# All eight x tiles of block 1 by DMA transpose, W1 stores spread over ten units, the sums of W1 tile 6 later in their period

## The chip, the cores and the metric

The kernel runs on one core of one Trainium2 chip. The metric is the device time of one execution in microseconds (us). A profile is one such execution, and its span, from the first to the last instruction, is about 1.8 us shorter than the time. Engines: PE (TensorE matmul), PEld (its weight loads), DVE (VectorE), ACT (ScalarE), POOL (GpSimd), SP (SyncE, which here only issues DMAs).

## The reference

```python
batch, m, k, h, n = 16, 512, 768, 3072, 768        # all float32
y = np.matmul(x, w1) + b1
y = 0.5 * y * (1.0 + erf(y / np.sqrt(2.0)))
return np.matmul(y, w2)
```

## The kernel before

The 8192 rows of x are worked in eight blocks of 1024 rows. Both matrix products use Strassen's scheme in its Winograd form: seven products of half-size blocks in place of eight, at the price of sums of operands on DVE. The first product goes unit by unit: unit (block, k) makes one pair of 128-wide column strips of the hidden layer. Blocks 0 and 1 are interleaved, since W1 is read from memory, cast and summed only once, and the finished W1 tiles (raw and summed, 672 KB each) are stored to DRAM for the later blocks. The order of units is:

```python
seq = ([(0, k) for k in range(7)] +
       [(1, 0), (1, 1), (1, 2), (0, 7), (1, 3), (0, 8), (1, 4), (0, 9), (1, 6), ...])
at = {u: n for n, u in enumerate(seq)}             # position; at[1, 0] is 7
```

Each position is one period of about 4.5 us. Within it, PE works on the unit `i` that starts and on the unit `j` before it, and calls `fill(slot)` between products. DVE executes in the order in which the program emits, so a slot decides what stands ahead of what:

```python
def period(i, j, fill):                            # cut
    p1(i, 0, i.C); copy_xy(i)                      # PE into bX; ACT
    p7(j)                                          # PE into bY, then DVE add (L613)
    fill(1)
    p5(i)                                          # PE into bW; ACT copy
    fill(2)
    p3(j)                                          # PE into bZ, then DVE add (L641)
    fill(3)
    p6(i)                                          # PE into bY, then DVE copy bY to bZ (L659)
    j.right_done(); fill(4)
    p4(j); fill(5)
    p2(i); fill(6)
```

The next period's `p7` accumulates in the same bY, so PE can't start it before the copy at L659 has read bY.

The sums wait in a list, `soon`. `sums(ns)` emits from its front as many as fit a budget, and slot 6 emits the rest. The parts that the change touches:

```python
X1_PE = (3, 7)                                     # these two x tiles are transposed on PE
X1_AT = ((5, 2), (6, 1))                           # at (position, slot)

KEEP = {at[1, 0]: range(7), at[0, 7] + 1: (7,), at[0, 8]: (8,), at[0, 9]: (9,), ...}

def transposes_a(pos):
    for t in (pos - 1, pos + 3):
        if t not in X1_PE:
            transpose_dma(1, t)                    # SP issues it (L305)

def fill_a(pos, slot):                             # cut
    if (pos, slot) in X1_AT:
        transpose_pe(1, X1_PE[X1_AT.index((pos, slot))])
    if pos == at[1, 0] - 1 and slot == 2:
        x_sums(1, soon, slice(RH // 2, RH), (0, 1))          # second half of the columns
    if slot == (1 if pos < at[1, 0] else 4) and pos + 1 < len(seq) and seq[pos + 1][0] == 0:
        prep_wt(seq[pos + 1][1])                   # four sums of the next W1 tile
    if slot == 1:
        if pos == at[1, 0] - 2:
            x_sums(1, soon, slice(0, RH // 2), (0, 1))       # first half: tiles 0, 1, 4, 5
    ...
    elif slot in (1, 2, 4, 5):
        sums((0, 600, 300, 0, 600, 300)[slot])
    if slot == 5:
        loads_a(pos)                               # POOL issues loads of W1, W2 and x
        if pos < 5:
            transposes_a(pos)
        for n in KEEP.get(pos, ()):
            keep(n)                                # SP stores W1 tile n (L225)
    if slot == 6:
        flush(soon)
```

Of the kernel before, what the change touches and what calls it, by code (L numbers as in the profile page):

```python
# [10 lines left out]
P = 128  # L11
# [11 lines left out]
def kernel(  # L23
# [8 lines left out]
    nc = tc.nc  # L32
    B, M, K = x.shape
# [6 lines left out]
    KQ = K // P // 2  # L40
# [48 lines left out]
    def cut(off, n, pattern=None, **dims):  # L89
        ap = arena[:, off:off + n]  # L90
        return ap.rearrange(pattern, **dims) if pattern else ap
# [94 lines left out]
    with tc.manual_schedule():  # L186
# [9 lines left out]
        def sums(ns):  # L196

            for q in (soon, queue):
                while q and ns >= q[0][0] * 0.6:
                    ns -= q[0][0]  # L200
                    q.pop(0)[1]()
# [25 lines left out]
        def prep_wt(n, ks=()):  # L227
            o = {s: w1_op(wts[n], s) for s in range(7)}
            early = ((T3, B22, T1, SUB), (T2, T3, B11, ADD), (T4, B21, T2, SUB), (T1, T1, B11, SUB))
            usual = ((T3, B22, T1, SUB), (T1, T1, B11, SUB), (T2, B22, T1, SUB), (T4, B21, T2, SUB))  # L230
            for d, a, b, op in [early[k] for k in ks] if ks else usual:
                later(KQ * P, lambda d=d, a=a, b=b, op=op: tt(o[d], o[a], o[b], op), soon)
# [6 lines left out]
        def prep_w2(d, c, q):  # L239
            a, b = {T1: (T3, B11), T2: (B22, T1), T3: (B22, T3), T4: (B21, T2)}[d]  # L240
            o = [w2v[s][:, :, c:c + W2C, :] for s in (d, a, b)]
            later(2 * W2C * N4, lambda: tt(*o, SUB), q)
# [47 lines left out]
        xhs = {}  # L290

        def xh_of(sb, t):
            if sb < ONE:
                return cut(sb * GR + GR // 2 + t * K, K)
            return xh_late[t % 3]
# [5 lines left out]
        def xT_of(sb, t):  # L301
            return XTs[sb][:, t // NU, :, (t % NU) * P:(t % NU + 1) * P]

        def transpose_dma(sb, t):
            nc.sync.dma_start_transpose(out=xT_of(sb, t), in_=xhs[t])  # L305

        def copy_halves(out, in_):
            for c in (slice(0, KQ), slice(KQ, 2 * KQ)):
                nc.scalar.copy(out=out[:, c, :], in_=in_[:, c, :])

        def transpose_pe(sb, t, copy=nc.scalar.copy):
            for kc in range(2 * KQ):
                nc.tensor.transpose(out=bT[t % 2][:, kc, :], in_=xhs[t][:, kc * P:(kc + 1) * P],
                                    identity=ident[:])
            copy(out=xT_of(sb, t), in_=bT[t % 2][:])
# [5 lines left out]
        def x_sums(sb, q, r=slice(0, RH), ks=range(4)):  # L321
            A11, A12, A21, A22 = [a[:, :, r] for a in blocks(sb)]
            S1, S2, S4 = [a[:, :, r] for a in XSs[sb]]
            n = KQ * len(range(RH)[r])
            ops = ((S1, A21, A22, ADD), (S2, S1, A11, SUB), (A21, A11, A21, SUB), (S4, A12, S2, SUB))
            for k in ks:
                later(n, lambda k=k: tt(*ops[k]), q)

        def g_sum(k, U, c0=0, c1=NH, q=None):
            G1, G2 = g_of(U // NU)  # L330
            r = slice(U % NU * P, (U % NU + 1) * P)
            g11, g21 = G1[:, c0:c1, 0, r], G1[:, c0:c1, 1, r]
            g12, g22 = G2[:, c0:c1, 0, r], G2[:, c0:c1, 1, r]
            s = [t[:, c0:c1, :] for t in GS]
            a, b, op = ((g21, g22, ADD), (s[0], g11, SUB), (g11, g21, SUB), (g12, s[1], SUB))[k]
            later((c1 - c0) * P, lambda: tt(s[k], a, b, op), q)
# [376 lines left out]
        xf = cut(GR, 8 * K).bitcast(FP32).rearrange("p (t k) -> p t k", t=4)  # L713
# [23 lines left out]
        def spin(n):  # L737

            for k in range(n):
                nc.tensor.matmul(out=(bX[1], bY[1])[k % 2][:], lhsT=zero[:, 0, 0:P], rhs=zero[:, 0, :],  # L740
                                 start=True, stop=True, skip_group_check=True)

        spin(9)
        for t in range(4):
            xhs[t] = xh_of(0, t)
            nc.vector.tensor_copy(out=xhs[t], in_=xf[:, t, :])
            transpose_pe(0, t, copy_halves if t == 3 else nc.scalar.copy)
            if t == 0:
                nc.tensor.transpose(out=bW[:, 0:2 * NH], in_=bf, identity=idf[0:2 * NH, 0:2 * NH])
                nc.scalar.copy(out=b1t[:], in_=bW[:, 0:2 * NH])  # L750
            spin(2)
# [7 lines left out]
        def plain(n, row, side, half, r=slice(0, RH)):  # L759
            slot = ((B11, T1), (B21, B22))[half][side]  # L760
            for c in range(KQ):
                nc.tensor.matmul(out=banks[n, row][side][:, r], lhsT=w1_op(wts[n], slot)[:, c, :],
                                 rhs=blocks(0)[2 * row + half][:, c, r],
                                 start=half == 0 and c == 0 and r.start == 0,
                                 stop=half == 1 and c == KQ - 1, skip_group_check=True)

        def plain_done(n, row, side):
            nc.scalar.activation(out=Gs[0][side][:, n, row, :], in_=banks[n, row][side][:, 0:RH],
                                 func=GELU, bias=b1t[:, 2 * n + side:2 * n + side + 1])
# [41 lines left out]
        for k in (2, 3):  # L811
            for r in (top, bottom):
# [5 lines left out]
        seq = ([(0, k) for k in range(7)] +  # L818
               [(1, 0), (1, 1), (1, 2), (0, 7), (1, 3), (0, 8), (1, 4), (0, 9), (1, 6), (0, 10), (0, 11),
                (1, 5), (1, 10), (1, 11), (1, 7), (1, 8), (1, 9)])  # L820
        at = {u: n for n, u in enumerate(seq)}
# [10 lines left out]
        def loads_a(pos):  # L832
            if pos == 0:
                load_wt(4)
                load_next_x(1, (0, 4, 1, 5))
                load_wt(5)
                load_next_x(1, (2, 6, 3, 7))
                load_wt(6)
            for n in range(7, NH):
                if pos == at[1, over[n]] + 1:  # L840
                    load_wt(n)
            if pos in w2_at_pos:
                load_w2(*w2_at_pos[pos])

        X1_PE = (3, 7)
        X1_AT = ((5, 2), (6, 1))

        KEEP = {at[1, 0]: range(7), at[0, 7] + 1: (7,), at[0, 8]: (8,), at[0, 9]: (9,), at[0, 10]: (10,), at[0, 11]: (11,)}

        def transposes_a(pos):  # L850
            for t in (pos - 1, pos + 3):
                if t not in X1_PE:
                    transpose_dma(1, t)

        def fill_a(pos, slot):
            if pos == 2 and slot == 1:
                plain(1, 1, 1, 1, bottom)
                plain_done(1, 1, 1)
            if (pos, slot) in X1_AT:
                transpose_pe(1, X1_PE[X1_AT.index((pos, slot))])  # L860
            if pos == at[1, 0] - 1 and slot == 2:
                x_sums(1, soon, slice(RH // 2, RH), (0, 1))
            if slot == (1 if pos < at[1, 0] else 4) and pos + 1 < len(seq) and seq[pos + 1][0] == 0:
                prep_wt(seq[pos + 1][1])
            if slot == 4:
                if pos in (3, 4):
                    prep_wt(pos - 3, (3,))
                for m, c in ((21, 9), (22, 0), (23, 3), (23, 6)):
                    if pos == m:
                        prep_w2(T2, c, queue)  # L870
                        prep_w2(T3, c, late if m == 23 else queue)
                if pos == 23:
                    for c in range(0, NH, W2C):
                        prep_w2(T4, c, late)
            if slot == 1:
                if pos == at[1, 0] - 2:
                    x_sums(1, soon, slice(0, RH // 2), (0, 1))
                if pos == at[1, 0]:
                    x_sums(1, soon, ks=(2, 3))
                if pos == at[0, NH - 1] + 2:  # L880
                    for c in range(0, NH, W2C):
                        prep_w2(T1, c, queue)
                    for k in (0, 1):
                        g_sum(k, 0)
            if pos > at[0, NH - 1]:
                if slot in (1, 4):
                    sums((0, 1100, 0, 0, 1500)[slot])
# [3 lines that stand above are left out]
                loads_a(pos)  # L891
# [3 lines that stand above are left out]
                    keep(n)  # L895
            if slot == 6:
                flush(soon)
# [231 lines left out]
```

## Time and profile before

| | before |
|---|---|
| time, median of six runs | 852.68 us (852.26 to 852.90) |
| span of the profile | 850.6 us |
| PE busy | 845.5 us, 99% |
| DVE, ACT busy | 78%, 50% |

From the page of the kernel before: its first line, PE's row of busy times, and the chain of waits by engine.

```profile
span 850.6 us, 16487 instructions
...
PE 845.5 (99%) x6432; PEld 569.6 (67%) x6432; DVE 667.2 (78%) x1126; ACT 421.3 (50%) x686; POOL 84.1 (10%) x135
...
PE 95%; DMA 4%; DVE 0%; ACT 0%; issue 0%; POOL 0%; DVEq 0%; ACTq 0%
```

PE is the bottleneck, but its busy time doesn't tell how much is left to gain. The Trainium skill says so in "Trainium Kernel Development and Optimization", section "Performance Expectations": matmul busy time is a bad metric, as matmuls are pipelined. So I used the starts: from the start of one matmul to the start of the next, minus its columns over 2.4 per ns (in the rows below six matmuls of 512 columns take 1.29 us, which is 2.4 columns per ns). What is left is called a **late start** here. In the kernel before they sum to 20.5 us: about 0.23 us in every 20 us of the first product (2.5 ns on each of its matmuls), 3.7 us in the first 20 us, while the first loads arrive, and then only one over 0.2 us before 300 us. That one is at 38.3 us.

DVE around it, from the timeline of the kernel before (start us, duration us, engine, line, operation, operands, shape, count, and in brackets the idle time before and what ended it; arena is the SBUF tensor with x, W1 and their sums, bX, bY, bZ, bW and bT are banks of PSUM):

```profile
34.54 0.69 DVE L613 TENSOR_TENSOR arena<-bY,arena 128x512 f32<-128x512 f32 x1 [0.86 <-PE bY L388]
36.14 1.14 DVE L191 TENSOR_TENSOR arena<-arena 128x384 f16<-128x384 f16 x3 [0.90 <-DMA arena<-in_w_dram]
37.20 0.68 DVE L641 TENSOR_TENSOR arena<-bZ,arena 128x512 f32<-128x512 f32 x1
37.99 0.70 DVE L659 COPY bZ<-bY 128x512 f32<-128x512 f32 x1
38.59 1.41 DVE L191 TENSOR_TENSOR arena<-arena 128x384 f16<-128x384 f16 x3
```

The three 128x384 operations at 36.14 us are sums of W1 tile 6. They waited 0.90 us for its load. L641 and L659 stand behind them. The last row, merged and named by its first form, holds the fourth W1 sum and the two x sums over the first half of the columns.

PE, from the same timeline:

```profile
34.92 0.50 PE L313 MATMUL bT<-ident,arena 128*128 128x128 f16 x6
...
37.20 1.46 PE L388 MATMUL bX<-arena 128*128 128x512 f16 x6
38.74 0.81 PE L388 MATMUL bY<-arena 128*128 128x512 f16 x3
39.38 0.50 PE L313 MATMUL bT<-ident,arena 128*128 128x128 f16 x6
...
42.31 1.46 PE L388 MATMUL bX<-arena 128*128 128x512 f16 x6
43.60 0.81 PE L388 MATMUL bY<-arena 128*128 128x512 f16 x3
```

Six matmuls of 512 columns take 1.29 us from start to start, so bY at 38.74 us is 0.25 us late, behind L659. The bT rows are the PE transposes that the change takes away: 0.34 us each, from their start to that of the next group.

SP's issues, from the timeline:

```profile
22.94 14.82 SPq L305 DMA_TRANSPOSE arena<-arena  x6
37.86 20.23 SPq L225 DMA_DIRECT2D w1s<-arena  x8
```

SP issues without waiting for PE's position: the stores of W1 follow directly behind the transposes. From the semaphore records of the trace, the transposes landed as follows (x tiles in the order of issue):

```
x tile      0      4      1      5      2      6
issued  22.94  24.38  25.72  31.77  34.80  36.38 us
landed  33.23  36.29  36.94  38.51  40.72  41.33 us
```

### The profile page before, as it was taken

To read this page: it belongs to the slowest core of one execution; us is meant where nothing else is said; L and a number is where in the kernel's file an instruction comes from. 1 tells how busy PE (TensorE), PEld (TensorE's weight loads), DVE (VectorE), ACT (ScalarE), POOL (GpSimd) and SP (SyncE) were. 2 spreads that over 40 slices of the span, in tenths; PEclk is the share of its full clock that TensorE was granted. 3 is DMA by queue.
4 is the path that set the end of the run, shared out by engine and by line. 5 is a ranking of instruction groups with operands and counts; after the bars stand their busy time and mean duration, and the time that the engine had idled before them with its cause. 6 is when DMAs were issued, how large, how long until landed. Compare 5 with 4: busy or idle time off the path is not lost.

```text
span 850.6 us, 16487 instructions
## 1 busy us (share of the span) xinstructions
PE 845.5 (99%) x6432; PEld 569.6 (67%) x6432; DVE 667.2 (78%) x1126; ACT 421.3 (50%) x686; POOL 84.1 (10%) x135
## 2 busy tenths in 40 slices
PE   9999999999999999999999999999999999999998
PEld 5444446687544897449964499645995469944798
DVE  5766678786657998679976799768996699956998
ACT  4777761122277513773148822487216771267611
POOL 5021100002100002000020000210002100010000
PEclk9999999999999999999999999999999999999999
DMA  9998777659999699987999689995999949984398
GB/s 229 199 284 170 165 160 277 234 195 218 234 331 207 194 332 372 296 177 236 332 381 266 155 291 335 361 293 111 315 351 344 283 111 328 356 311 172 101 310 283
DMA packets 143522, 219.05 MB, mean 258 GB/s; under 512 B 61756, under 2 KB 84724, under 8 KB 143444
## 3 DMA queue, kind: packets, MB, share of 16 engines
q1 hardware_dynamic: 117824, 179.74, 67.3%
q0 software_dynamic: 25440, 38.15, 20.6%
q8 instruction: 50, 0.82, 0.4%
q14 instruction: 28, 0.23, 0.1%
q10 hardware_dynamic: 180, 0.11, 0.0%
HBM read 180.30 MB, written 47.87 MB: 268 GB/s over the span
## 4 chain that ended last, share of the span: by engine, by line
PE 95%; DMA 4%; DVE 0%; ACT 0%; issue 0%; POOL 0%; DVEq 0%; ACTq 0%
PE bY L388 21%; PE bY L493 15%; PE bX L388 14%; PE bX L493 10%; PE bZ L388 7%; PE bW L388 7%; PE bZ L493 5%; PE bW L493 5%; PE bY L432 5%; DMA arena<-in_x_dram 2%; PE bZ L432 2%; PE bW L432 2%; PE bX L432 2%; DMA arena<-in_w_dram 1%; PE bY L580 1%; PE bX L580 1%
## 5 line engine op out<-in xcount | busy, mean ns | idle before, releaser
L191 DVE TENSOR_TENSOR arena<-arena 128x768 f16<-128x768 f16 (+4 forms) x630 | 403.4, 671 | 7.5 <-PE bW L432 1.1
L388 PEld LDWEIGHTS <-arena 128*128 128x128 f16 x1974 | 192.6, 98 | 224.0 <-issue 0.4
L493 PEld LDWEIGHTS <-arena 128*128 128x128 f16 x3528 | 292.1, 98 | 8.4 <-issue 0.4
L388 PE MATMUL bY<-arena 128*128 128x512 f16 x846 | 214.4, 379 | 0.1
L613 DVE TENSOR_TENSOR arena<-bY,arena 128x512 f32<-128x512 f32 (+1 forms) x102 | 69.4, 681 | 127.0 <-PE bY L388 90.3
L493 PE MATMUL bY<-arena 128*128 128x192 f16 x1500 | 138.3, 246 | 0.0
L388 PE MATMUL bX<-arena 128*128 128x512 f16 x564 | 138.2, 379 | 0.0
L606 ACT COPY bY<-bX 128x512 f32<-128x512 f32 (+1 forms) x143 | 78.6, 550 | 119.4 <-DVE arena L542 82.0
L404 ACT ACTIVATE arena<-arena,b1t 128x1024 f16<-128x1024 f32 x94 | 108.0, 1149 | 54.0 <-DVE arena L641 54.0
L626 ACT COPY arena<-bW 128x512 f32<-128x512 f32 (+1 forms) x147 | 81.1, 552 | 90.7 <-PE bW L493 43.9
L493 PE MATMUL bX<-arena 128*128 128x192 f16 x1020 | 93.1, 246 | 0.1
L641 DVE TENSOR_TENSOR arena<-bZ,arena 128x512 f32<-128x512 f32 (+1 forms) x102 | 69.3, 679 | 22.2 <-PE bZ L388 18.2
L388 PE MATMUL bW<-arena 128*128 128x512 f16 x282 | 76.2, 379 | 0.0
L388 PE MATMUL bZ<-arena 128*128 128x512 f16 x282 | 76.2, 379 | 0.0
L432 PEld LDWEIGHTS <-arena 128*128 128x128 f16 x528 | 51.6, 98 | 34.1 <-issue 0.2
L525 POOL DMA_DIRECT2D out_dram<-arena x42 | 30.6, 729 | 406.4 <-DVE arena L637 370.2
L409 ACT ACTIVATE arena<-bX,b1t 128x512 f16<-128x512 f32 x94 | 64.0, 681 | 10.0 <-PE bX L388 10.0
L409 ACT ACTIVATE arena<-bY,b1t 128x512 f16<-128x512 f32 x94 | 63.4, 674 | 0.0
L657 ACT COPY bZ<-bY 128x512 f32<-128x512 f32 (+1 forms) x54 | 29.0, 537 | 65.7 <-DVE arena L641 31.4
L299 POOL DMA_DIRECT2D arena<-in_x_dram x60 | 32.7, 550 | 248.2 <-DMA arena<-arena 137.9
L493 PE MATMUL bW<-arena 128*128 128x192 f16 x504 | 48.4, 246 | 0.0
L493 PE MATMUL bZ<-arena 128*128 128x192 f16 x504 | 48.4, 246 | 0.0
(60 smaller groups left out, 401.8 us busy)
## 6 DMA issues: line engine op xcount, KB each, us to landing
arena<-w2s SPq DMA_DIRECT2D x294, 288.0 KB, 4.7
arena<-w1s SPq DMA_DIRECT2D x72, 672.0 KB, 7.0
out_dram<-arena POOLq DMA_DIRECT2D x42, 384.0 KB, 7.2
w2s<-arena SPq DMA_DIRECT2D x49, 288.0 KB, 3.8
arena<-in_x_dram POOLq DMA_DIRECT2D x60, 192.0 KB, 7.1
w1s<-arena SPq DMA_DIRECT2D x12, 672.0 KB, 6.1
arena<-in_w_dram POOLq DMA_DIRECT2D x17, 384.0 KB, 7.6
out_dram<-arena SPq DMA_DIRECT2D x17, 384.0 KB, 3.4
```

Source lines behind the costliest of these rows:

```text
L191: nc.vector.tensor_tensor(out=o, in0=a, in1=b, op=op)
L299: nc.gpsimd.dma_start(out=xhs[t], in_=xr[:, sb * 8 + t, :])
L388: nc.tensor.matmul(out=dst[:, 0:RH], lhsT=w1_op(self.wt, slot)[:, c, :], rhs=a[:, c, :], start=first and c == 0, stop=c == self.C - 1, ski ...
L404: nc.scalar.activation(out=self.G[1][:, hi, :, :], in_=self.tmp, func=GELU, bias=b1t[:, 2 * hi + 1:2 * hi + 2])
L409: nc.scalar.activation(out=self.G[0][:, hi, row, :], in_=bank[:, 0:RH], func=GELU, bias=b1t[:, 2 * hi:2 * hi + 1])
L432: nc.tensor.matmul(out=dst[:, 0:N2], lhsT=a, rhs=w[:, :, c, :], start=first and c == 0, stop=c == self.C - 1, skip_group_check=True)
L493: nc.tensor.matmul(out=dst[:, t * N4:(t + 1) * N4], lhsT=a, rhs=w[:, c, :], start=first and c == 0 and t == ts[0], stop=c == NQ - 1, skip_ ...
L525: eng.dma_start(out=orr[:, s0:s0 + 2, right * N2:(right + 1) * N2], in_=self.dst[:, r].rearrange("p t h n -> p t (h n)"))
L606: nc.scalar.copy(out=bY[u.g % 2][:, 0:u.F], in_=bX[u.g % 2][:, 0:u.F])
L613: nc.vector.tensor_tensor(out=u.c22(), in0=bY[u.g % 2][:, 0:u.F], in1=w[:, 0:u.F], op=ADD)
L626: nc.scalar.copy(out=w[:, 0:u.F], in_=bW[:, 0:u.F])
L641: nc.vector.tensor_tensor(out=u.c12(), in0=bZ[:, 0:u.F], in1=w[:, 0:u.F], op=ADD)
```

## The change

Its intent: take the last 12 PE transposes off the bottleneck; let the sums of W1 tile 6 no longer hold back L641 and L659 while they wait for their load; spread the W1 stores, seven of which went out at once; and let the first real matmul start a little sooner, by casting x tile 3 of block 0 in two halves. The sums over the second half of block 1's x move from slot 2 to slot 4, as the added transposes land later.

```diff
-            nc.vector.tensor_copy(out=xhs[t], in_=xf[:, t, :])
+            if t < 3:
+                nc.vector.tensor_copy(out=xhs[t], in_=xf[:, t, :])
+            else:
+                nc.vector.tensor_copy(out=xhs[t][:, 0:KH], in_=xf[:, t, 0:KH])
+                nc.vector.tensor_copy(out=xhs[t][:, KH:K], in_=xf[:, t, KH:K])
...
-        X1_PE = (3, 7)
-        X1_AT = ((5, 2), (6, 1))
-        KEEP = {at[1, 0]: range(7), at[0, 7] + 1: (7,), at[0, 8]: (8,), at[0, 9]: (9,), at[0, 10]: (10,), at[0, 11]: (11,)}
+        KEEP = {7: (0, 1), 9: (2,), 10: (3,), 12: (7, 4), 13: (5,), 14: (8,), 15: (6,), 16: (9,), 17: (10,), 18: (11,)}
...
-                if t not in X1_PE:
-                    transpose_dma(1, t)
+                transpose_dma(1, t)
...
-            if (pos, slot) in X1_AT:
-                transpose_pe(1, X1_PE[X1_AT.index((pos, slot))])
-            if pos == at[1, 0] - 1 and slot == 2:
+            if pos == at[1, 0] - 1 and slot == 4:
                 x_sums(1, soon, slice(RH // 2, RH), (0, 1))
-            if slot == (1 if pos < at[1, 0] else 4) and pos + 1 < len(seq) and seq[pos + 1][0] == 0:
+            if slot == (1 if pos < at[1, 0] - 2 else 4) and pos + 1 < len(seq) and seq[pos + 1][0] == 0:
                 prep_wt(seq[pos + 1][1])
```

In the changed kernel the lines stand a little lower: L388 is L390 there, L613 is L615, L641 is L643, L659 is L661.

More of the change, by code (lines that the diff above doesn't have):

```diff
@@ L309, in copy_halves @@
                 nc.scalar.copy(out=out[:, c, :], in_=in_[:, c, :])
+        KH = KQ * P
         def transpose_pe(sb, t, copy=nc.scalar.copy):
```

## The prediction

> **What bounds the kernel.** TensorE. The page gives PE 99% busy at clock 1.0; the chain of waits is 95% PE. Busy time hides stalls, so I took the starts of successive matmuls from the timeline and subtracted (columns written)/2.4 per ns. Beyond a background of 0.23 us per 20 us, the first 120 us lose only: about 3 us in the first 10 us, of which the change can touch 0.30 us (at 9.0 us the first real matmul waits for ScalarE's copy of x tile 3, L309), and 0.25 us at 38.3 us (bY waits for VectorE's copy L659). There is little to win.
>
> **What the change removes.**
> - Two groups of six PE transposes (x tiles 3 and 7 of block 1), at 34.92 and 39.38 us in the timeline: 0.34 us each. Two ScalarE copies of 0.81 us go too; ScalarE is not critical.
> - The 0.25 us stall: VectorE sat from 35.2 to 36.14 us waiting for W1 tile 6, which delayed L641 and L659. Those sums now come after L659.
> - Casting tile 3 in halves starts its transposes about 0.3 us sooner, but the transposes of tiles 5 and 6 already wait for their loads (gaps of about 0.2 us at 13.7 and 14.6 us): I keep 0.1 us.
> - The W1 stores cost PE nothing: no matmul between 45 and 120 us starts late. SP issues without regard to PE's position, so stores 0 to 3 still go out together, directly after the transposes.
>
> **What it adds and moves.** Two more DMA transposes at the end of SP's queue, from about 37.9 us (1.3 us of issue each, 3 to 5 us to landing): tile 3 lands near 42.7, tile 7 near 44 us. Their first users come at about 43 us, close.
>
> Worse: without the W1 sums ahead of them, the two sums over the first half of block 1's x move from 38.6 to about 35.2 us on VectorE, ahead of L641 and L659. The first reads x tiles 4 and 5, and the transpose of tile 5 (fourth in the queue) landed at 38.51 us. Before, that wait was covered. The queue is slow there: about 120 of its 256-byte packets per us at 27 to 31 us beside the W1 and x loads, about 1,000 per us after 36 us. This agrees with the Trainium skill, "DMA: Bandwidth & Descriptors", section "Queues, rings and completion order": engines alternate between queues packet by packet. Nothing in the change makes tile 5 land earlier.
>
> So on VectorE: wait 35.2 to 38.5, two sums (0.47 us apart) until 39.5, L641, L659 until about 41.0. PE's next bY group (38.74 us before) starts at 41.03: 2.3 us later, plus perhaps 0.1 us for the sum T1 of W1 tile 6, queued behind L659.
>
> **Sum.** +2.3 +0.1 (the stall absorbs the earlier savings: start, first transpose group, 0.25 us) -0.34 (second transpose group) = +2.0 us: 852.8 becomes 854.8 us, all of it before 45 us; afterwards the traces should match, shifted by 2 us.
>
> **Range** 852.2 to 855.9. Faster by over 2%: 0.01; within 2%: 0.98; slower by over 2%: 0.01.
>
> **Right if** VectorE shows a wait of about 3 us before 128x768 sums from 35 to 38.5 us, released by a DMA transpose, and PE a gap of about 2.7 us near 38 us before bY, released by L659; no bT matmuls from 30 to 45 us; no late matmuls from 50 to 120 us.
>
> **Wrong if** the fourth transpose lands before 36 us (then 851.6 to 852: all savings kept), or tiles 3 and 7 land after 45 us (over 856), or the moved stores delay W1 tiles 7 to 11.

## The result, and the profile after

The time rose by about 2 us: 854.79 us median of six runs (854.29 to 856.63), against 852.68 us. The ratio is 1.0029 (95% interval 1.0017 to 1.0042), slower beyond doubt. The slowest of the six, 856.63 us, shows a mean granted clock of 0.998 where the others show 1.000; what that means is seen in an experiment below. Ratios here are the mean time of one kernel's runs over that of the other's of the same rounds, so not quite the ratio of the medians.

The page of the kernel after:

```profile
span 854.0 us, 16465 instructions
...
PE 844.3 (99%) x6420; PEld 568.2 (67%) x6420; DVE 667.5 (78%) x1127; ACT 419.9 (49%) x684; POOL 83.6 (10%) x135
...
PE 94%; DMA 3%; SPq 1%; DVE 0%; issue 0%; ACT 0%; DVEq 0%; ACTq 0%
```

PE has 12 matmuls fewer and is busy 1.2 us less, in a span that is 3.3 us longer.

DVE in the same stretch, from the timeline of the kernel after:

```profile
34.98 0.69 DVE L615 TENSOR_TENSOR arena<-bY,arena 128x512 f32<-128x512 f32 x1 [0.86 <-PE bY L390]
38.29 1.15 DVE L191 TENSOR_TENSOR arena<-arena 128x768 f16<-128x768 f16 x2 [2.62 <-DMA arena<-arena]
39.36 0.68 DVE L643 TENSOR_TENSOR arena<-bZ,arena 128x512 f32<-128x512 f32 x1
40.15 0.70 DVE L661 COPY bZ<-bY 128x512 f32<-128x512 f32 x1
40.76 1.52 DVE L191 TENSOR_TENSOR arena<-arena 128x384 f16<-128x384 f16 x4
```

The two x sums (128x768) now come first and wait 2.62 us for a DMA from arena to arena, which is a transpose. The four W1 sums run at the end, without any wait. The wait for a load became a longer wait for a transpose.

PE after, with a later stretch of the same timeline in the last three rows:

```profile
37.30 1.46 PE L390 MATMUL bX<-arena 128*128 128x512 f16 x6
40.90 0.81 PE L390 MATMUL bY<-arena 128*128 128x512 f16 x3 [2.15 <-DVE bZ L661]
...
44.21 1.46 PE L390 MATMUL bX<-arena 128*128 128x512 f16 x6
45.51 0.81 PE L390 MATMUL bY<-arena 128*128 128x512 f16 x3
...
74.64 1.46 PE L390 MATMUL bY<-arena 128*128 128x512 f16 x6
75.94 0.81 PE L390 MATMUL bX<-arena 128*128 128x512 f16 x3
77.93 0.82 PE L390 MATMUL bX<-arena 128*128 128x512 f16 x3 [1.18 <-DMA arena<-in_w_dram]
```

bY starts at 40.90 us, where it started at 38.74 us before: 2.16 us later. One period on, with the second group of PE transposes gone, the distance is 45.51 - 43.60 = 1.91 us. At 77.93 us there is a second late start, of 1.35 us, which I had not predicted: PE waits for W1 tile 9. The 1.91 us and these 1.35 us, together 3.26 us, are the difference of the two spans but for 0.07 us.

SP after:

```profile
23.53 18.14 SPq L305 DMA_TRANSPOSE arena<-arena  x8
41.77 18.22 SPq L225 DMA_DIRECT2D w1s<-arena  x5
```

```
x tile      0      4      1      5      2      6      3      7
issued  23.53  24.96  26.30  32.31  35.34  36.86  38.19  40.43 us
landed  33.78  36.75  37.41  38.20  40.24  41.69  42.40  43.20 us
```

DVE's wait ended at 38.29 us, with the landing of x tile 5 at 38.20 us. That transpose is the fourth, as before, and it landed no later than before.

### The profile page after: what moved, and what is told of

It reads as the page before. It is cut to its first block, busy times and chain, and to the rows that moved or that the text cites. A ratio compares the mean times of both kernels' runs of the same rounds, so it can differ in the third digit from the quotient of the medians.

```text
span 854.0 us, 16465 instructions
## 1 busy us (share of the span) xinstructions
PE 844.3 (99%) x6420; PEld 568.2 (67%) x6420; DVE 667.5 (78%) x1127; ACT 419.9 (49%) x684; POOL 83.6 (10%) x135
## 4 chain that ended last, share of the span: by engine, by line
PE 94%; DMA 3%; SPq 1%; DVE 0%; issue 0%; ACT 0%; DVEq 0%; ACTq 0%
PE bY L390 20%; PE bY L495 15%; PE bX L390 13%; PE bX L495 10%; PE bZ L390 7%; PE bW L390 7%; PE bZ L495 5%; PE bW L495 5%; PE bY L434 5%; DMA arena<-in_w_dram 3%; PE bZ L434 2%; PE bW L434 2%; PE bX L434 2%; PE bY L582 1%; SPq L305 1%; PE bX L582 1%
## 5 line engine op out<-in xcount | busy, mean ns | idle before, releaser
L390 PEld LDWEIGHTS <-arena 128*128 128x128 f16 x1974 | 192.4, 98 | 228.3 <-issue 2.6
L390 PE MATMUL bY<-arena 128*128 128x512 f16 x846 | 214.4, 379 | 2.1 <-DVE bZ L661 2.1
L615 DVE TENSOR_TENSOR arena<-bY,arena 128x512 f32<-128x512 f32 (+1 forms) x102 | 69.4, 680 | 127.1 <-PE bY L390 89.9
L390 PE MATMUL bX<-arena 128*128 128x512 f16 x564 | 138.4, 379 | 1.2 <-DMA arena<-in_w_dram 1.2
L643 DVE TENSOR_TENSOR arena<-bZ,arena 128x512 f32<-128x512 f32 (+1 forms) x102 | 69.3, 679 | 22.4 <-PE bZ L390 18.4
L390 PE MATMUL bW<-arena 128*128 128x512 f16 x282 | 76.2, 379 | 0.0
L390 PE MATMUL bZ<-arena 128*128 128x512 f16 x282 | 76.2, 379 | 0.0
L659 ACT COPY bZ<-bY 128x512 f32<-128x512 f32 (+1 forms) x54 | 29.0, 537 | 65.0 <-DVE arena L643 31.2
```

Source lines behind the costliest of these rows:

```text
L390: nc.tensor.matmul(out=dst[:, 0:RH], lhsT=w1_op(self.wt, slot)[:, c, :], rhs=a[:, c, :], start=first and c == 0, stop=c == self.C - 1, ski ...
L615: nc.vector.tensor_tensor(out=u.c22(), in0=bY[u.g % 2][:, 0:u.F], in1=w[:, 0:u.F], op=ADD)
L643: nc.vector.tensor_tensor(out=u.c12(), in0=bZ[:, 0:u.F], in1=w[:, 0:u.F], op=ADD)
```

## The experiments

All twelve medians, with that of the kernel before on the same chip, and the late starts over 0.2 us between 20 and 120 us of the one profile that each run gave ("at" is the start of the matmul before the late one):

| run | median us | before us | ratio (95% interval) | late starts: at us, size us |
|---|---|---|---|---|
| after | 854.79 | 852.68 | 1.0029 (1.0017, 1.0042) | 38.4: 2.31; 76.4: 1.35 |
| after_again | 854.51 | 853.10 | 1.0020 (1.0008, 1.0033) | 38.0: 2.61 |
| sums_only | 854.33 | 852.61 | 1.0019 (1.0007, 1.0032) | 39.6: 1.18 |
| stores_only | 852.88 | 852.61 | 1.0002 (0.9989, 1.0015) | none |
| cast_only | 853.00 | 853.10 | 0.9998 (0.9986, 1.0011) | none |
| transposes_only | 855.45 | 852.58 | 1.0026 (1.0012, 1.0040) | 38.5: 0.33; 56.4: 2.54; seven at the low clock |
| sums_back | 852.48 | 852.61 | 0.9998 (0.9985, 1.0010) | none |
| stores_back | 854.82 | 852.61 | 1.0027 (1.0013, 1.0040) | 38.7: 1.86; 58.1: 0.53 |
| sums_stores_back | 856.66 | 853.10 | 1.0036 (1.0023, 1.0050) | 38.5: 0.71; 56.8: 2.73; eight at the low clock |
| x_sums_later | 852.23 | 853.10 | 0.9993 (0.9980, 1.0005) | 43.3: 0.39 |
| x_sums_again | 852.58 | 852.58 | 0.9999 (0.9987, 1.0012) | 43.3: 0.25 |
| singly | 852.35 | 852.58 | 0.9997 (0.9984, 1.0009) | none |

Every experiment gave a correct result. The first real matmul started anywhere from 9.3 to 10.9 us in these profiles, following the landing of the first x and W1 loads; a difference of some tenths between two medians is therefore not a finding.

### sums_back: the W1 sums in front again

```diff
-            if slot == (1 if pos < at[1, 0] - 2 else 4) and ...
+            if slot == (1 if pos < at[1, 0] else 4) and ...
```

> The changed kernel with one part undone: the W1 tile 6 sums go back ahead of the x sums. My theory (the two x sums, left first in VectorE's order, wait for the DMA transpose of x tile 5 and hold back L643 and L661): VectorE no longer waits about 2.6 us for a transpose near 36 us, the bY group after the first X group near 38 us starts at most 0.3 us late, and the time falls by about 2 us, to 852.2 to 853.2 us (more only if W1 tile 9 is late, as in the profile after). Rival (eight DMA transposes on a slow queue, or the moved stores, cost the 2 us, whatever the order of the sums): the gap near 38 us stays over 1 us and the time stays over 854 us.

852.48 us: the 2 us are gone. The timeline of DVE in this run:

```profile
36.13 1.14 DVE L191 TENSOR_TENSOR arena<-arena 128x384 f16<-128x384 f16 x3 [0.30 <-DMA arena<-in_w_dram]
37.19 0.68 DVE L643 TENSOR_TENSOR arena<-bZ,arena 128x512 f32<-128x512 f32 x1
37.98 0.70 DVE L661 COPY bZ<-bY 128x512 f32<-128x512 f32 x1
38.58 1.41 DVE L191 TENSOR_TENSOR arena<-arena 128x384 f16<-128x384 f16 x3
```

PE in the same run starts its bY group 1.29 us after the first bX matmul, on time:

```profile
37.46 1.46 PE L390 MATMUL bX<-arena 128*128 128x512 f16 x6
38.75 0.81 PE L390 MATMUL bY<-arena 128*128 128x512 f16 x3
```

The x sums are again behind L661, and tile 5 landed at 38.70 us, later than in the run after. The same slow transpose, and no late start: it isn't the speed of the transposes that cost time, it is the place of the first sum that reads them. The rival falls. From the first real matmul's start to the last's, this profile takes 836.1 us against 837.2 us before: the rest of the change seems to save about 1.1 us on PE (one profile each), near the 0.68 us of the transposes and the 0.25 us of the late start, but the median shows only 0.1 us of it.

### sums_only: the W1 sums later, nothing else

The same line as above, changed in the kernel before.

> The kernel before with the later W1 tile 6 sums alone; six DMA transposes, PE transposes of x tiles 3 and 7, old stores. My theory: the wait of about 3 us on VectorE before the 128x768 sums and the PE gap near 38 us of about 2.0 us appear here too, with no added transpose: +2.2 us, 854.5 to 855.3 us. Rival (the gap comes from the two added DMA transposes): no gap, the 0.25 us stall of before is gone, 852.3 to 852.7 us.

854.33 us, +1.7 us, with six DMA transposes and the PE transposes in place. DVE and PE in this run:

```profile
38.44 1.15 DVE L191 TENSOR_TENSOR arena<-arena 128x768 f16<-128x768 f16 x2 [1.83 <-DMA arena<-arena]
39.51 0.68 DVE L641 TENSOR_TENSOR arena<-bZ,arena 128x512 f32<-128x512 f32 x1
40.29 0.70 DVE L659 COPY bZ<-bY 128x512 f32<-128x512 f32 x1
```

```profile
38.57 1.46 PE L388 MATMUL bX<-arena 128*128 128x512 f16 x6
41.05 0.81 PE L388 MATMUL bY<-arena 128*128 128x512 f16 x3 [1.02 <-DVE bZ L659]
```

The gap is there without the added transposes, so they don't cause it. It is smaller than I expected (1.18 us, not 2.0), because this execution's first real matmul came at 10.9 us, 0.9 us later than in the run after, and because the first group of PE transposes (0.34 us) still stands before the gap. bY starts about 2.7 us after the landing of tile 5 (38.34 us here), nearly all of it DVE work, so whatever PE gains or loses before that moment is swallowed. In the four profiles with the late W1 sums behind the early x sums, bY starts at 40.74 to 41.05 us, while the first real matmul moves between 9.3 and 10.9 us.

### x_sums_later: the waiting sums moved too

```diff
-            if slot == 1:
-                if pos == at[1, 0] - 2:
-                    x_sums(1, soon, slice(0, RH // 2), (0, 1))
+            if pos == at[1, 0] - 2 and slot == 4:
+                x_sums(1, soon, slice(0, RH // 2), (0, 1))
+            if slot == 1:
```

> The changed kernel, but the two sums over the first half of x of block 1 also move, behind L661 of their period and behind the W1 sums. Theory (only the order of the waiting sums against L643 and L661 costs time): the VectorE wait of 2.6 us and the PE gap of 2.3 us go; six sums in a row behind L661 may hold later steps back by 0.3 to 0.6 us near 39 to 44 us; 852.2 to 853.0 us. Rival (W1 sums behind L661 are themselves the cost, whatever waits ahead of them): over 854 us.

852.23 us, 0.9 us under the median of before on that chip, with an interval that includes 1. DVE:

```profile
37.12 0.70 DVE L661 COPY bZ<-bY 128x512 f32<-128x512 f32 x1 [0.51 <-DVE arena L643]
37.73 2.59 DVE L191 TENSOR_TENSOR arena<-arena 128x384 f16<-128x384 f16 x6
...
43.33 1.15 DVE L191 TENSOR_TENSOR arena<-arena 128x768 f16<-128x768 f16 x2 [1.01 <-DMA arena<-arena]
```

L661 runs at 37.12 us, the earliest of all, with the W1 sums behind it: they do no harm there, so the rival falls. What stays late is the second half of the x sums, which waits for x tile 7 until 43.33 us (0.39 us for PE). A second set of rounds:

> The run with the first-half x sums behind L661 a second time, as its interval against before (0.998 to 1.0005) left open whether it is faster. If it is: median 0.3 to 0.9 us under before on this chip and 852.0 to 852.5 us. If not: within 0.2 us of before. In its profile: no gap near 38 us, at most 0.5 us late near 43 us.

852.58 us, exactly the median of before: not faster as far as the time tells. From the first real to the last matmul, its profile takes 836.6 us and that of x_sums_later 836.5 us, against 837.2 us before. The 0.6 to 0.7 us saved are visible there, but they are within the scatter of the start.

### stores_back and stores_only: the W1 stores

```diff
-        KEEP = {7: (0, 1), 9: (2,), 10: (3,), 12: (7, 4), 13: (5,), 14: (8,), 15: (6,), 16: (9,), 17: (10,), 18: (11,)}
+        KEEP = {at[1, 0]: range(7), at[0, 7] + 1: (7,), at[0, 8]: (8,), at[0, 9]: (9,), at[0, 10]: (10,), at[0, 11]: (11,)}
```

> The changed kernel with the W1 stores of before. The profile after shows a second late start, 1.35 us at 76 us, where PE waits for W1 tile 9, which landed 16.4 us after its issue instead of 9.1. If the moved stores (tiles 7, 4, 5, 8, 6 from 60 to 78 us) cause it: no late start between 60 and 80 us, tile 9 lands about 9 us after its issue, the gap near 38 us stays at about 2.3 us, and the median falls by at most 0.7 us (most timed runs after seem not to have the late tile): 854.0 to 854.8 us. Rival (the late tile was chance on the memory side): tile 9 varies here as well, and the time is that of after.

> The kernel before with the moved W1 stores alone. If the moved stores delay W1 tile 9: tile 9 lands over 12 us after its issue and PE starts up to 1.4 us late near 75 us; 852.7 to 854.0 us. Rival (stores cost PE nothing, as my prediction said): no late start between 50 and 120 us, 852.5 to 852.9 us.

Neither moved the time: 854.82 us against 854.79 us after, and 852.88 us against 852.61 us before. But the loads of W1 tiles 7 and 9 do move. Issue to landing, in us, from the trace:

```
                    stores       last of the first    W1 tile 7        W1 tile 9
                                 stores landed        issue landed     issue landed
before              together     53.0                 50.5   56.1      59.6   68.7
stores_back         together     55.6                 52.3   58.8      61.9   69.7
stores_only         spread       48.0                 51.0   55.9      60.1   73.6
after               spread       50.1                 52.4   57.7      61.5   77.9
after_again         spread       50.1                 52.3   57.2      61.4   76.6
sums_back           spread       50.3                 50.3   55.1      59.3   73.1
x_sums_later        spread       50.4                 50.2   55.1      59.3   73.0
```

With the stores spread, SP sends those of tiles 7, 4 and 5 together near 59 us, just ahead of the load of tile 9, which takes 14 to 16 us in place of 8 to 9. PE needs tile 9 near 76.6 us in the kernel after: one profile shows it 1.35 us late, the other shows no late start over 0.2 us, and nor do the other profiles with the stores spread in this way show one there (stores_only, sums_back, x_sums_later, x_sums_again), though tile 9 takes about 14 us in them. In stores_back it is tile 7 that is late (0.53 us). So spreading the stores moves the slow load from tile 7 to tile 9, where PE mostly has time for it.

### sums_stores_back and transposes_only: the stores beside eight transposes

sums_stores_back is the changed kernel with both lines above undone. transposes_only is the kernel before with

```diff
-        X1_PE = (3, 7)
-        X1_AT = ((5, 2), (6, 1))
+        X1_PE, X1_AT = (), ()
...
-            if pos == at[1, 0] - 1 and slot == 2:
+            if pos == at[1, 0] - 1 and slot == 4:
```

> The changed kernel with both the W1 tile 6 sums and the W1 stores as before: what is left is the half cast and eight DMA transposes. Theory: with no VectorE wait near 36 us and no moved stores, removing 12 PE transposes (0.68 us) pays: no late start over 0.3 us from 20 to 120 us, 851.8 to 852.5 us, 0.1 to 0.8 us under before. Rival (eight DMA transposes give back what they save, by landing late at unit (1,0)): late starts near 42 to 44 us of 0.3 us or more and 852.5 to 853 us.

> The kernel before with all eight x tiles of block 1 by DMA transpose (and the second half of the x sums in slot 4, as the change has them), W1 stores, W1 sums and cast as before. Theory from the run with sums and stores back: two more transposes put the block of seven stores about 4 us later on SP's queue, they land until about 56 us instead of 53, W1 tile 7 lands 7 to 9 us after its issue instead of 5.5, near 59 us, and PE waits 1.5 to 3 us for it near 57 us: 854.5 to 857 us. Rival (that run's loss came from the half cast or from a bad chip state): no late start near 57 us, 852.0 to 852.6 us.

I expected the first to be the best kernel. It is the slowest, 856.66 us, and transposes_only (855.45 us) confirms why. PE in sums_stores_back:

```profile
56.34 0.81 PE L390 MATMUL bX<-arena 128*128 128x512 f16 x3
59.72 0.90 PE L390 MATMUL bX<-arena 128*128 128x512 f16 x3 [2.57 <-DMA arena<-in_w_dram]
60.41 1.48 PE L390 MATMUL bY<-arena 128*128 128x512 f16 x3
61.69 1.48 PE L390 MATMUL bW<-arena 128*128 128x512 f16 x3
```

and in transposes_only:

```profile
59.19 1.03 PE L388 MATMUL bX<-arena 128*128 128x512 f16 x2 [2.37 <-DMA arena<-in_w_dram]
```

PE waits for W1 tile 7. In transposes_only the two added transposes put the seven stores back to 41.8 us (37.9 us before), they land until 56.6 us, and tile 7, issued at 50.6 us, lands only at 59.1 us. With the stores spread (sums_back) only four stores stand there, they have landed by 50.3 us, and the same load, issued at 50.3 us, lands at 55.1 us. sums_back differs from sums_stores_back in the stores alone.

Then the clock drops. From the windows of sums_stores_back (stretch, its length, busy time and count of PE, PEld, DVE, ACT and POOL, granted clock, DMA share, GB/s):

```profile
56.00:60.00 4.00, 1.43 (x8) 0.47 (x7) 1.00 (x2) 2.27 (x3) 1.05 (x2) 1.00 1.25 194
60.00:64.00 4.00, 4.00 (x12) 1.42 (x11) 1.82 (x5) 1.16 (x2) 0.00 (x0) 0.57 1.31 209
```

Twelve matmuls in 4 us, where the next 16 us have 19 in every 4 us, at a granted clock of 0.57. Eight starts at the low clock are about 0.21 us late each, which adds 1.7 us to the 2.73 us. In transposes_only it is seven starts and 1.5 us, on top of 2.54 us. Not every execution pays this: a mean granted clock of 0.998, as these two profiled runs have it, stands in three of the five timed runs of sums_stores_back and in one of the five of transposes_only. The losses in both profiles are about four times what the change was meant to save (0.68 us of PE transposes, 0.25 us of the late start, and a little at the beginning).

### singly: each of the three late stores behind a later tile

```diff
-        KEEP = {7: (0, 1), 9: (2,), 10: (3,), 12: (7, 4), 13: (5,), 14: (8,), 15: (6,), 16: (9,), 17: (10,), 18: (11,)}
+        KEEP = {7: (0, 1), 9: (2,), 10: (3,), 12: (7,), 13: (8, 4), 15: (9, 6), 16: (10, 5), 18: (11,)}
```

on top of x_sums_later. As SP issues in order, a store of a tile whose sums aren't done holds back those behind it, and this spreads them in fact, not only in the program text: the store of tile 4 left at 67.18 us, behind that of tile 8 at 66.81 us, and not at 57.84 us as in x_sums_later.

> The changed kernel with the first-half x sums behind L661 (as in the run with the x sums later) and with the stores of W1 tiles 4, 5 and 6 each behind the store of a later tile, so that SP holds them back until that tile's sums are done. Theory (stores 4 and 5, issued right behind 7, share the DMA engines with the load of W1 tile 9): tile 9 lands 8 to 10 us after its issue, not 13 to 17; no late start from 50 to 120 us; the median is that of the x sums later, 852.0 to 852.6 us. Rival (tile 9 is late for another reason): still over 12 us.

Tile 9 landed 9.0 us after its issue (59.6 to 68.6 us), and there is no late start over 0.2 us from 20 to 120 us. The median, 852.35 us, is 0.2 us under before, within the interval. In x_sums_later, which differs in the stores alone, tile 9 took 13.7 us. This confirms that the stores issued just ahead of it, those of tiles 4 and 5, had delayed tile 9. It is the calmest version, not a measurably faster one.

### cast_only and after_again

cast_only is the kernel before with the half cast of the change's first hunk.

> The kernel before with x tile 3 cast in halves, nothing else. Theory: the first real matmul is gated by loads whose landing varies by over 1 us between executions; the half cast gains at most 0.2 us: 852.3 to 852.7 us, same as before within the interval. Rival (the extra VectorE instruction delays the W1 cast behind it): 852.8 to 853.2 us.

853.00 us against 853.10 us: nothing either way. The median lies in the rival's range, but so does that of before on this chip, so the ranges in us decide nothing here.

> The changed kernel, unaltered, a second time. Theory: the gap near 38 us, released by L661, is there in every execution, 1.8 to 2.4 us (smaller where the first real matmul starts later), and the median is again 854.3 to 855.0 us. The late start near 76 us for W1 tile 9 is a matter of margin: tile 9 lands 13 to 17 us after its issue in every execution, but makes PE wait only in some. Rival: the late start near 76 us is in every execution; then it must show again with over 1 us.

854.51 us. The gap near 38 us is there again, 2.61 us, with an early first matmul (9.3 us). PE in this run:

```profile
40.80 0.81 PE L390 MATMUL bY<-arena 128*128 128x512 f16 x3 [2.45 <-DVE bZ L661]
```

The late tile 9 is not there: it landed at 76.6 us, 15.2 us after its issue, and PE was 0.12 us late for it. So the second late start of the first profile is a matter of margin, as my theory had it, and the typical loss of 2 us is that of the first.

## Why the prediction was right

The time was predicted as 854.8 us and is 854.79 us. The mechanism is the one predicted; that the sum met the median to a hundredth is luck, since one term in it was set to zero wrongly and others vary by tenths (2.4 us was predicted for the gap and 0.34 us to be won back after it; measured were 2.16 and 0.25 us).

- **The wait on DVE.** Predicted from 35.2 to 38.5 us on the transpose of x tile 5; measured from about 35.7 to 38.29 us (2.62 us), released by a DMA transpose. sums_only shows that the moved W1 sums alone cause it, and sums_back that undoing them ends it.
- **PE's bY.** Predicted at 41.03 us, measured at 40.90 us, released by L661. The late start of 2.31 us is less than the predicted 2.7 us because this execution started about 0.5 us later; the wait swallows the difference.
- **After it.** Predicted +2.0 us behind the second transpose group; measured +1.91 us.
- **x tiles 3 and 7.** Predicted to land near 42.7 and 44 us; measured 42.40 and 43.20 us, in time behind the gap. Without the gap they can be tight: 0.39 us late in x_sums_later, nothing over 0.2 us in sums_back.
- **The half cast.** Predicted 0.1 us, swallowed; cast_only shows nothing measurable.
- **The W1 stores: the step that failed.** The prediction said "The W1 stores cost PE nothing" and expected no late matmul from 50 to 120 us. Of the kernel before this is right (stores_only: +0.02%, with an interval of 0.13% to either side). Of the changed kernel it is not. The spread is what makes eight DMA transposes affordable: without it, W1 tile 7 comes 2.5 to 2.7 us late (transposes_only, sums_stores_back). And it moves the slow load to tile 9, which took 16.4 us in the kernel after in place of 9.1 us and was 1.35 us late in one of two profiles. The prediction had named "the moved stores delay W1 tiles 7 to 11" among the things that would make it wrong; that happened to tile 9, but a second run of the same kernel (after_again) lost only 0.12 us to it. I had looked at the stores as they stood before, when two more transposes in front of them on the same queue were about to move them by 4 us. The prediction escaped in part because the gap at 38 us also gives the loads 2 us more time: in stores_back the late start for tile 7 is only 0.53 us.

What stays open is why a load beside stores is so slow. In transposes_only the packet records show none of the load queue before 55.7 us, 5.1 us after POOL issued the load of tile 7, while store packets ran; in sums_back, with the stores done, its packets started 1.55 us after the issue. In four profiles with the stores together (before, stores_back, transposes_only, sums_stores_back) the first load packet came 0.16 to 0.21 us before the last packet of these stores, so tile 7 waited for them to drain. But later, in the kernel after, loads and stores ran side by side (72 load and 60 store packets between 67 and 68 us). I have not tested what decides this.

## What to carry to other kernels

Before you move work out of the way of an in-order engine, look at what then stands first in that engine's order and what it waits for: here a sum that had waited 0.9 us hid a sum that would have waited 2.6 us. Judge several parts of a change together, since one part can be free alone and costly (or indispensable) beside another, as here the transposes and the stores on one in-order DMA queue. On a saturated engine measure start-to-start gaps, not busy time, and count a gap's aftermath on the clock as well.

## What the Trainium skill lacked or had wrong

- "TensorE: Matmul & The Clock Gate", section "Why this matters for your kernels", asks for no PE idle gaps over about 3 us, and its Part 1 gives an idle window of about 3.4 us, free-running. Here 2.57 us idle (sums_stores_back) and 2.37 us (transposes_only) were already followed by eight and seven matmuls of 512 columns at about half speed (0.57 granted over 4 us in the first). 2.45 us idle in after_again was not: the clock stayed at 1.00. The page's limit of 3 us is too generous here. That one gap is punished and a longer one is not fits a free-running window: the stretches in the traces' clock records are whole multiples of 3.4133 us (in both punished runs 54.61 us, 16 of them, at full clock, then one at half; 846.5 and 849.9 us, 248 and 249 of them, at full clock in after_again and after). Cut at these boundaries, the punished gaps have 2.57 and 2.01 us in one stretch of 3.41 us, and the unpunished ones at most 1.81 us (after; 1.68 us in after_again). So less than a whole idle window was enough in these two profiles; where the line lies between 1.81 and 2.01 us, and whether this share is what counts, no run tests.
- "DMA: Bandwidth & Descriptors", section "Queues, rings and completion order", says that each DMA engine alternates between queues packet by packet. Transposes and loads did share the engines about one packet to one (in the kernel before, 126 transpose and 109 load packets from 28 to 29 us, 215 and 236 from 32 to 33 us; with the loads gone, 1,036 transpose packets from 36 to 37 us and about 500 per us in the next two). But beside the 672 KB stores the load queue started no packet for 5.1 us after its issue (transposes_only), against 1.55 us without them (sums_back). SP's queue, while loads ran, shows such waits too: the first transpose moved no packet for 4.1 us after its issue and the store of tile 7 none for 4.3 us (before); that the loads cause these was not tested. The section gives no hint that a queue can wait so long for its first packet beside another.
- The same page gives a bandwidth for DMA transposes, but no duration for one of a 128x768 tile of 2-byte elements from SBUF to SBUF. In the kernel before SP needed 1.2 to 6.0 us to issue one (median 1.2 us), and it landed 2.7 to 11.9 us after its issue (median 5.1 us); the longest, 10.3 to 11.9 us, are the first three of block 1, beside loads.
